# A tile of its own for the gate's normalized product, three weight stores moved from block 0 to block 1, and split z weights read back

## The chip, the cores and the metric

The kernel runs on one core of a Trainium2 chip. The metric is the device time of one execution in microseconds (us), the median of several runs.

## What is computed

One layer of a streaming encoder, for 2048 new prompt frames and 32 frames of a running stream (with 2048 cached keys and values). Cut to what matters here:

```python
def mixer(h, k_past, v_past, ssm_h0, conv_prev, p):
    proj = h @ p['w_in']                       # q, k, v, z, xbc, dt
    ...
    attn = stick_breaking(q, q_pos, k_all, v_all, k_pos).reshape(b, l, D_ATT)
    xbc_c, conv_new = causal_dwconv(xbc, conv_prev, p['ssm_conv_w'], p['ssm_conv_b'])
    xbc_c = jax.nn.silu(xbc_c)                 # x (4 tiles of 128), B, C
    ...
    y, h_fin = ssd_scan(xh, dt, a, bm, cm, ssm_h0.astype(jnp.float32))
    y = y + p['d_skip'].astype(jnp.float32)[:, None] * xh
    y = rmsnorm(y * jax.nn.silu(z), p['g_ssm_out'])      # the gate
    out = jnp.concatenate([rmsnorm(attn, p['g_attn_out']), y], axis=-1) @ p['w_out']
    return out, k, v, h_fin.astype(ssm_h0.dtype), conv_new

def layer(x, ...):
    x = x + rmsnorm(mixer(rmsnorm(x, p['g_mix_pre']), ...), p['g_mix_post'])
    x = x + rmsnorm(conv_ffn(rmsnorm(x, p['g_ffn_pre']), ...), p['g_ffn_post'])
```

## The kernel before

Frames lie along the free axis, features on the 128 partitions. The 2080 frames are cut into four blocks (`SBS`): 512, 512, 512 and 544 frames, numbered 0 to 3 (`s`).

Precision. Every fp32 operand of a matmul is split into a high part (rounded to fp32r) and a low part (the rest), and three matmuls (high x high, high x low, low x high) make one product; `dense` (L169) issues them. A weight that comes from its input tensor is loaded raw (L130), the high part is a cast on ScalarE (ACT, L153) and the low part a subtraction on GpSimd (POOL, L154), both in `divide`. If `divide` is given a key, the split pair is stored to a scratch tensor in device memory (L157), and the next `weight` call with that key reads it back with one load (`recall`, L145). A split pair has twice the bytes of the raw weights. All loads and stores are issued by SyncE (SP) in one order.

The input phase (`phase_in`) handles the four blocks one after another, with weight units of 8 chunks of 128 x 128, three buffers for split pairs and two for raw weights. In a block it projects tiles 4 and 5 (B and C), then 0 to 3 (x), each followed by the causal convolution on VectorE (DVE, L400, L404) into `bc` or `xc` and a SiLU (L384 on ACT, L385 on DVE); `xc` has one buffer, used by all blocks in turn. The copies of the projections out of PSUM (L393, L395) are on ACT. Then come V (L428; its weights `wvhi`, `wvlo` are split while block 0 runs, L291 and L292; copies L435 and L437), the state scan (L506 to L580), K and Q (L169; copy L360, split L602, L603), and the gate: `gate` multiplies the scan's output in `xc` with SiLU of the z projection (L652), `gate_norm` takes the root mean square (L663 to L667, `rstd`), multiplies by it (L672, in place in `xc`), splits the product (`khi` L676 on ACT, `klo` L678 on POOL) and stores both parts (L679, L680).

Block 3's `gate` and `gate_norm` are not run in the input phase: they are the filler of the attention of block 0 (`heads`), one step per slot. From there on weight units are of 4 chunks, with six buffers for split pairs and five for raw weights. In a slot PE makes scores (L885, L889), ACT two sigmoids (L733, L734), DVE a product scan (`prow`, L736), POOL or DVE a product (L741), PE transposes (L904) and the product with V (L926). The 32 frames of the running stream (`sample`, L759 to L800) are woven in, with their own loads of cached keys and values. PE's order is fixed here by pins between neighbours (`pin`, `mark`); the order on other engines, and in the input phase on all, comes from the scheduler of the framework, which lays out the whole program at compile time by simulating it.

The attention of block s + 1 is then woven with the output projection and the feed-forward network of block s (`Tail`). The change doesn't touch these.

Of the kernel before, what the change touches and what calls it, by code (L numbers as in the profile page):

```python
# [8 lines left out]
F32 = mybir.dt.float32  # L9
# [3 lines left out]
ALU = mybir.AluOpType  # L13
# [5 lines left out]
UNIT = 4  # L19
# [12 lines left out]
P = 128  # L32
# [13 lines left out]
NSB = len(SBS)  # L46
# [6 lines left out]
C_GSSM = 36  # L53
# [12 lines left out]
def tiles_of(n):  # L66
    return [(0, n)] if n <= 512 else [(0, n // 2), (n // 2, n)]


class Kernel:  # L70
# [69 lines left out]
    def recall(self, pool, keys, m, tag=None):  # L140

        w = self.held(pool, tag)
        q = m // len(keys)
        for i, k in enumerate(keys):
            self.nc.sync.dma_start(w[:, :, q * i : q * i + q, :].bitcast(F32), self.kept[k][:])  # L145
        return [(w[:, 0, i, :], w[:, 1, i, :]) for i in range(m)]

    def divide(self, pool, raw, m, key=None, tag=None):

        nc = self.nc  # L150
        w = self.held(pool, tag)
        hi, lo = w[:, 0, :m, :], w[:, 1, :m, :]
        nc.scalar.copy(hi, raw[:, :m, :])  # L153
        nc.gpsimd.tensor_tensor(lo, raw[:, :m, :], hi.bitcast(F32), op=ALU.subtract)  # L154
        if key is not None:
            d = self.kept[key] = self.dp.tile([P, 2, m, P], F32, name="wS_" + "_".join(map(str, key)))
            nc.sync.dma_start(d[:], w[:, :, :m, :].bitcast(F32))  # L157
        return [(w[:, 0, i, :], w[:, 1, i, :]) for i in range(m)]

    def parts(self):  # L160
# [19 lines left out]
    def rstd(self, pool, psp, sq, n, width, tag="rstd", pt="st"):  # L180
        nc = self.nc
        r = pool.tile([P, 544], F32, name=tag)
        for c0, c1 in tiles_of(n):
            ps = psp.tile([P, 512], F32, name=pt)
            nc.tensor.matmul(
                ps[:, : c1 - c0], self.ones[:], sq[:, c0:c1], start=True, stop=True
            )
            nc.scalar.activation(
                r[:, c0:c1], ps[:, : c1 - c0], AF.Sqrt, bias=self.eps[:], scale=1.0 / width
            )  # L190
        nc.vector.reciprocal(r[:, :n], r[:, :n])
        return r
# [68 lines left out]
def phase_in(kn, ctx):  # L261
    nc, tc, a, o = kn.nc, kn.tc, kn.a, kn.o
# [7 lines left out]
    wp = kn.wp  # L270
# [88 lines left out]
        else:  # L359
            nc.scalar.copy(dst, ps)  # L360

    wfirst = kn.weight(wp, a["wbx"][4], key=("bx", 4))
    for s, (t0, nt) in enumerate(SBS):
        last = s == NSB - 1
        if s == 0:
# [6 lines left out]
        xc = kn.xcp.tile([P, 4, 547], F32, name="xc")  # L372
# [9 lines left out]
        def silu(y, copy):  # L382
            t = tmp.tile([P, 550], F32, name="t")
            kn.behind(nc.scalar.activation(t[:, :W], y, AF.Sigmoid), copy)  # L384
            nc.vector.tensor_tensor(y, y, t[:, :W], op=ALU.mult)  # L385

        for c in (4, 5, 0, 1, 2, 3):
            w = wfirst if s == 0 and c == 4 else kn.weight(wp, a["wbx"][c], key=("bx", c))
            for c0, c1 in tiles_of(nt):
                ps = psd.tile([P, 512], F32, name="o")  # L390
                kn.dense(ps, w, xs, c0, c1)
                e = min(c1, 512)
                copy = nc.scalar.copy(raw[:, c, 3 + c0 : 3 + e], ps[:, : e - c0])  # L393
                if c1 > 512:
                    copy = nc.scalar.copy(raw[:, c, 518:550], ps[:, e - c0 : c1 - c0])  # L395
            if s == 0:
                nc.vector.tensor_tensor(raw[:, c, 3 : 3 + nt], raw[:, c, 3 : 3 + nt], r0[:, :nt], op=ALU.mult)
            y = xc[:, c, :W] if c < 4 else bc[:, c - 4, :W]
            wc = C_SW + c * 4
            nc.vector.tensor_scalar(  # L400
                y, raw[:, c, 0:W], kn.col(wc), kn.col(C_SB + c), op0=ALU.mult, op1=ALU.add
            )
            for i in range(1, 4):
                nc.vector.scalar_tensor_tensor(  # L404
                    y, raw[:, c, i : i + W], kn.col(wc + i), y, op0=ALU.mult, op1=ALU.add
                )
            if owed is not None:
                silu(owed, copy)
            owed = y
# [12 lines left out]
        for b in range(nb):  # L422
            q = min(P, nt - b * P)
# [67 lines left out]
        for b in range(nb):  # L491
            q = min(P, nt - b * P)
# [12 lines left out]
            for h in range(NH):  # L505
                nc.vector.tensor_scalar(  # L506
                    acB[:q, h, :q], acB[:q, h, :q], acum[:q, b * 8 + h : b * 8 + h + 1], 0.0,
                    op0=ALU.subtract, op1=ALU.min,
# [82 lines left out]
        for name, dst in (("wk", kn.kS), ("wq", kn.qS)):  # L591
            for c in range(4):
                w = kn.weight(wp, a[name][c])
                hi = so.tile([P, 544], F32, name="khi")[:].bitcast(F32R)
                lo = so.tile([P, 544], F32, name="klo")[:].bitcast(F32R)
                kf = so.tile([P, 544], F32, name="kf")
                for c0, c1 in tiles_of(nt):
                    ps = psd.tile([P, 512], F32, name="o")
                    kn.dense(ps, w, xs, c0, c1)
                    n = c1 - c0  # L600
# [13 lines left out]
        if last:  # L614
            return lambda tm, pool: (
                gate(kn, s, xs, xc, None, tm),
                gate_norm(kn, s, xc, tm, lambda sq, *r: kn.rstd_narrow(pool, *kn.bank, [sq], *r)),
            )
        bufs = {"khi": 2, "klo": 2, "t": 2, "sq": 1, "zc": 2}
        tm = lambda nm: (so if nm in ("khi", "klo") else tmp).tile([P, 550 if nm == "t" else 544], F32, name=nm, bufs=bufs[nm])  # L620
        for _ in gate(kn, s, xs, xc, r0 if s == 0 else None, tm):
            pass
        for _ in gate_norm(kn, s, xc, tm, lambda *r: kn.rstd(rp, psm, *r, tag="rstd2")):
            pass


def gate(kn, s, xs, xc, r0, tm):

    nc, nt = kn.nc, SBS[s][1]
    tiles = tiles_of(nt)  # L630
    for c in range(4):
        w = kn.weight(kn.wp, kn.a["wz"][c], key=("z", c) if s < NSB - 1 else None)
        for c0, c1 in tiles:
            n = c1 - c0
            ps = kn.po.tile([P, 512], F32, name="o")
            for k in range(KC):
                kn.dense(ps, w[k : k + 1], xs, c0, c1, k0=k, first=k == 0, last=k == KC - 1, pin=s == NSB - 1)
                if len(tiles) == 1 or k % 2:
                    yield
            t = tm("t")  # L640
            if r0 is not None:
                z = tm("t")
                nc.vector.tensor_tensor(z[:, :n], ps[:, :n], r0[:, c0:c1], op=ALU.mult)
                ps = z
            elif s < NSB - 1:
                z = tm("zc")
                nc.scalar.copy(z[:, :n], ps[:, :n])
                ps = z
            nc.scalar.activation(t[:, :n], ps[:, :n], AF.Sigmoid)
            nc.vector.tensor_tensor(t[:, :n], ps[:, :n], t[:, :n], op=ALU.mult)  # L650
            e = min(c1, 512)
            nc.vector.tensor_tensor(xc[:, c, c0:e], xc[:, c, c0:e], t[:, : e - c0], op=ALU.mult)  # L652
            if c1 > 512:
                nc.gpsimd.tensor_tensor(xc[:, c, 512:544], xc[:, c, 515:547], t[:, e - c0 : n], op=ALU.mult)


def gate_norm(kn, s, xc, tm, rstd):

    nc, nt = kn.nc, SBS[s][1]
    sq = tm("sq")  # L660
    for c in range(4):
        if c == 0:
            nc.scalar.activation(sq[:, :nt], xc[:, c, :nt], AF.Square)  # L663
        else:
            t = tm("t")
            nc.scalar.activation(t[:, :nt], xc[:, c, :nt], AF.Square)
            nc.gpsimd.tensor_tensor(sq[:, :nt], sq[:, :nt], t[:, :nt], op=ALU.add)  # L667
        yield
    r = rstd(sq, nt, 512)
    for c in range(4):  # L670
        yield
        nc.vector.scalar_tensor_tensor(  # L672
            xc[:, c, :nt], xc[:, c, :nt], kn.col(C_GSSM + c), r[:, :nt], op0=ALU.mult, op1=ALU.mult
        )
        hi = tm("khi")[:, :nt].bitcast(F32R)
        nc.scalar.copy(hi, xc[:, c, :nt])  # L676
        lo = tm("klo")[:, :nt].bitcast(F32R)
        nc.gpsimd.tensor_tensor(lo, xc[:, c, :nt], hi.bitcast(F32), op=ALU.subtract)  # L678
        nc.sync.dma_start(kn.yS[s][0, :, c, :], hi.bitcast(F32))  # L679
        nc.sync.dma_start(kn.yS[s][1, :, c, :], lo.bitcast(F32))  # L680

# [281 lines left out]
class Tail:  # L963
# [187 lines left out]
    def sums(self, j, gate, up):  # L1151


        kn, nc = self.kn, self.kn.nc
        (a11, a12), (a21, a22) = gate, up
        op = lambda out, a, b, o: nc.vector.tensor_tensor(out[:], a[:], b[:], op=o)
        op(a11, a11, a21, ALU.subtract)
        op(a21, a21, a22, ALU.add)
        op(a22, a22, a11, ALU.subtract)
        op(a12, a12, a22, ALU.subtract)  # L1160
        return {7: a11, 5: a21, 6: a22, 3: a12}
# [332 lines left out]
def build(nc, tc, a, o):  # L1494
    kn = Kernel(nc, tc, a, o)
    with ExitStack() as ctx:
# [17 lines left out]
        with ExitStack() as c2:  # L1514
            kn.wp, kn.unit, kn.wbufs, kn.rbufs = c2.enter_context(tc.tile_pool(name="weights_in", bufs=1)), KC, 3, 2
            rest = phase_in(kn, c2)
# [125 lines left out]
```

## Time and profile before

| | before |
|---|---|
| median of 3 runs | 2924.41 us (2918.09 to 2925.8) |
| the profiled execution | 2923.97 us |
| its span, first to last instruction | 2922.2 us |
| mean granted TensorE clock | 0.981 |
| PE busy | 2808.3 us (96%) |
| DVE busy | 1667.7 us (57%) |
| ACT busy | 1246.6 us (43%) |
| POOL busy | 1203.1 us (41%) |
| moved by DMA | 610.59 MB |

The profiled execution is a run of its own; its time stands beside the span because some microseconds lie before the first and after the last instruction. A row of a timeline gives the start, the duration, the engine, the line, the operation, out<-in, shapes and how many are merged, and in brackets the idle time of the engine before it with what ended it. PE is TensorE's matmuls, PEld its weight loads. A row of waits gives who waited for whom: total, times, longest.

### The profile page before, as it was taken

Reading aid. Unit: us, or ns where it says so; the run is one execution under the profiler, and the core shown is the slowest. Engines: PE = TensorE matmul, PEld = TensorE weight load, DVE = VectorE, ACT = ScalarE, POOL = GpSimd, SP = SyncE. Lnnn points to the kernel's source line nnn. Section 1 sums busy time; section 2 is a strip of 40 time slices with the busy share of each in tenths; the row PEclk is TensorE's granted clock in tenths of the full one; section 3 lists DMA queues with packets and bytes.
Section 4 is the critical chain, followed back from the end, with each engine's and each line's share of the span. In section 5 each row is a group of like instructions: output and inputs, shape, how many; then the busy total and the mean of one; then the engine's idle time right before and its main releaser. Section 6 shows DMA issues by size and latency. Waiting matters only on the chain.

```text
span 2922.2 us, 46225 instructions
## 1 busy us (share of the span) xinstructions
PE 2808.3 (96%) x16771; PEld 2428.2 (83%) x16771; DVE 1667.7 (57%) x2628; ACT 1246.6 (43%) x2604; POOL 1203.1 (41%) x1105
## 2 busy tenths in 40 slices
PE   7999999989989999999999999989999999999998
PEld 6787878877878888897788888978888889899997
DVE  7666666557574555457555556676656663623333
ACT  4344344337565454455333334654444443321111
POOL 4535252335666666656322323453322223511113
PEclk9999999989889999999999999999999999999999
DMA  7766665658777778776755556666555555755556
GB/s 263 206 234 196 222 174 201 173 139 283 242 249 267 258 265 272 262 266 225 232 172 175 178 184 221 216 194 204 169 171 171 164 163 201 244 176 175 171 177 204
DMA packets 334533, 610.59 MB, mean 209 GB/s; under 512 B 73466, under 2 KB 192898, under 8 KB 329698
## 3 DMA queue, kind: packets, MB, share of 16 engines
q1 hardware_dynamic: 334306, 607.64, 64.2%
q8 instruction: 134, 2.20, 0.3%
q14 instruction: 93, 0.76, 0.1%
HBM read 459.33 MB, written 148.18 MB: 208 GB/s over the span
## 4 chain that ended last, share of the span: by engine, by line
PE 77%; DVE 10%; DMA 7%; issue 2%; ACT 2%; SPq 1%; POOL 1%; DVEq 0%; POOLq 0%; ACTq 0%
PE o L169 38%; PE u L169 12%; PE t L169 10%; PE z L885 4%; PE pa L926 4%; PE pt L904 3%; PE o L428 3%; DVE acB L506 1%; DVE xc L404 1%; DMA xr<-hS 1%; DVE prow L736 1%; DVE xc L560 1%; DMA w<-wS_up 1%; DMA acB<-acD 1%; DVE xlo L1074 1%
## 5 line engine op out<-in xcount | busy, mean ns | idle before, releaser
L169 PE MATMUL o<-xhi,w 128*128 128x512 f32 (+2 forms) x3968 | 1050.4, 346 | 21.8 <-ACT xhi L342 7.8
L169 PEld LDWEIGHTS o<-xhi,w 128*128 128x128 f32 x3968 | 700.8, 192 | 115.0 <-ACT xhi L342 7.8
L169 PE MATMUL o<-xlo,w 128*128 128x512 f32 (+2 forms) x1984 | 684.7, 345 | 2.1 <-DVE xlo L343 1.1
L741 POOL TENSOR_TENSOR beta<-beta,prow 128x512 f32<-128x512 f32 (+3 forms) x256 | 253.4, 991 | 450.0 <-DVE prow L736 376.1
L169 PEld LDWEIGHTS o<-xlo,w 128*128 128x128 f32 x1984 | 380.7, 192 | 45.1 <-DVE xlo L343 1.6
L154 POOL TENSOR_TENSOR w<-wraw,w 128x512 fp32r<-128x512 f32 (+3 forms) x218 | 313.9, 1443 | 206.9 <-ACT w L153 186.0
L169 PE MATMUL u<-xhi,w 128*128 128x512 f32 x1056 | 350.1, 397 | 0.0
L169 PE MATMUL o<-ah,w 128*128 128x512 f32 x992 | 344.1, 403 | 4.6 <-DVE f L1370 3.8
L1322 POOL TENSOR_TENSOR y<-y,gb 128x512 f32<-128x512 f32 (+1 forms) x88 | 115.9, 1317 | 503.1 <-ACT gb L1321 503.0
L736 DVE TENSOR_TENSOR_SCAN prow<-gam,prow,z 128x513 f32<-128x513 f32 x192 | 245.2, 1278 | 72.5 <-ACT beta L734 69.5
L909 DVE TENSOR_TENSOR wt<-pt,wt 128x512 fp32r<-128x512 f32 (+2 forms) x320 | 190.9, 602 | 160.1 <-ACT wt L908 158.4
L908 ACT CAST wt<-pt 128x512 fp32r<-128x512 f32 (+2 forms) x320 | 166.9, 527 | 222.2 <-PE pt L904 220.4
L169 PEld LDWEIGHTS u<-xhi,w 128*128 128x128 f32 x1056 | 199.2, 189 | 46.9
L169 PEld LDWEIGHTS o<-ah,w 128*128 128x128 f32 x992 | 187.0, 189 | 47.1 <-DVE f L1370 5.7
L153 ACT CAST w<-wraw 128x512 fp32r<-128x512 f32 (+3 forms) x218 | 145.1, 666 | 166.9 <-PE o L169 111.5
L733 ACT ACTIVATE gam<-z 128x512 f32<-128x512 f32 (+2 forms) x320 | 172.6, 539 | 95.2 <-PE z L885 54.8
L169 PE MATMUL u<-xlo,w 128*128 128x512 f32 x528 | 209.5, 397 | 0.0
L169 PE MATMUL o<-al,w 128*128 128x512 f32 x496 | 196.6, 396 | 0.0
L169 PE MATMUL t<-xhi,w 128*128 128x272 f32 x960 | 187.4, 291 | 2.6 <-DMA w<-wS_up 1.7
L904 PE MATMUL pt<-ident,beta 128*128 128x128 f32 x1088 | 181.3, 279 | 3.0 <-DVE beta L741 1.8
L1314 DVE SCALAR_TENSOR_TENSOR y<-gb,cv,y 128x512 f32<-128x512 f32 (+1 forms) x176 | 142.1, 808 | 73.4 <-ACT y L1312 70.7
L926 PE MATMUL pa<-wt,v 128*64 128x256 f32 (+3 forms) x1152 | 174.6, 282 | 8.9 <-DVE wt L909 6.8
(282 smaller groups left out, 4924.5 us busy)
## 6 DMA issues: line engine op xcount, KB each, us to landing
w<-wS_up SPq DMA_DIRECT2D x264, 512.0 KB, 3.6
w<-wS_dn SPq DMA_DIRECT2D x144, 384.0 KB, 3.5
wS_up<-w SPq DMA_DIRECT2D x88, 512.0 KB, 3.5
w<-wS_out SPq DMA_DIRECT2D x78, 512.0 KB, 5.8
wraw<-wup SPq DMA_DIRECT2D x88, 256.0 KB, 4.3
k<-kS SPq DMA_DIRECT2D x80, 256.0 KB, 4.0
v<-vS SPq DMA_DIRECT2D x80, 256.0 KB, 3.8
w<-wS_bx SPq DMA_DIRECT2D x18, 1024.0 KB, 4.8
```

Source lines behind the costliest of these rows:

```text
L153: nc.scalar.copy(hi, raw[:, :m, :])
L154: nc.gpsimd.tensor_tensor(lo, raw[:, :m, :], hi.bitcast(F32), op=ALU.subtract)
L169: mm = nc.tensor.matmul(ps[:, : c1 - c0], l, r, start=first and i == 0 and k == 0, stop=last and i == 2 and k == len(w) - 1, **({"skip_gro ...
L733: nc.scalar.activation(g[:, c0:512], z, AF.Sigmoid, scale=-0.125)
L736: nc.vector.tensor_tensor_scan(back(pr), back(g), z[:, 0:1].to_broadcast([P, n + 1]), self.kn.ones[:, 0:1] if prev is None else prev, op0= ...
L741: eng.tensor_tensor(b[:, :n], b[:, :n], pr[:, c0 + 1 : 513], op=ALU.mult)
L885: mm = nc.tensor.matmul(z[:, :n], q[:, P * b : P * b + P], k[:, :n], start=e == 0, stop=e == 1 and kc < s)
L904: mm = nc.tensor.transpose(t[:, P * j : P * j + P], w[:, P * j : P * j + P], kn.ident[:])
L908: nc.scalar.copy(hi, t)
L909: nc.vector.tensor_tensor(lo, t, hi.bitcast(F32), op=ALU.subtract)
L926: nc.tensor.matmul(av[:m, 2 * P * p + c0 : 2 * P * p + 2 * P], v[:, j, :m], wt[:, rest, j, c0:], start=kc == s and p + j + rest == 0, stop ...
L1314: nc.vector.scalar_tensor_tensor(y[:, :W], gb[:, i : i + W], kn.col(wc + i), y[:, :W], op0=ALU.mult, op1=ALU.add)
```

## The change

Three edits. The normalized product in `gate_norm` goes, for blocks 0 to 2, to a tile of its own (`zc`, two buffers) in place of `xc`; ACT and POOL read it there. The split weights of tiles 4, 5 and 0 of the B/C/x projection get no key in block 0, so they aren't stored there; block 1 loads them raw, splits them again and stores them, and blocks 2 and 3 read them back as before. Block 3's z weights, loaded raw and split in units of 4 chunks before, are read back as halves of the units of 8 chunks that block 0 stored; for that, `divide` also notes the parts of a long unit under keys of their own.

```diff
@@ recall
-            self.nc.sync.dma_start(w[:, :, q * i : q * i + q, :].bitcast(F32), self.kept[k][:])
+            self.nc.sync.dma_start(w[:, :, q * i : q * i + q, :].bitcast(F32), self.kept[k])
@@ divide
-            d = self.kept[key] = self.dp.tile([P, 2, m, P], F32, name="wS_" + "_".join(map(str, key)))
+            d = self.dp.tile([P, 2, m, P], F32, name="wS_" + "_".join(map(str, key)))
             nc.sync.dma_start(d[:], w[:, :, :m, :].bitcast(F32))
+            self.kept[key] = d[:]
+            if m > UNIT:
+                for i in range(0, m, UNIT):
+                    self.kept[(*key[:-1], "part", i)] = d[:, :, i : i + UNIT, :]
@@ phase_in
-    wfirst = kn.weight(wp, a["wbx"][4], key=("bx", 4))
+    wfirst = kn.weight(wp, a["wbx"][4])
...
         for c in (4, 5, 0, 1, 2, 3):
-            w = wfirst if s == 0 and c == 4 else kn.weight(wp, a["wbx"][c], key=("bx", c))
+            w = wfirst if s == 0 and c == 4 else kn.weight(wp, a["wbx"][c], key=("bx", c) if s or c in (1, 2, 3) else None)
@@ gate
     for c in range(4):
-        w = kn.weight(kn.wp, kn.a["wz"][c], key=("z", c) if s < NSB - 1 else None)
+        w = kn.weight(kn.wp, kn.a["wz"][c], key=("z", c) if s < NSB - 1 else ("z", c, "part"))
@@ gate_norm
     for c in range(4):
         yield
+        n = xc[:, c, :nt] if s == NSB - 1 else tm("zc")[:, :nt]
         nc.vector.scalar_tensor_tensor(
-            xc[:, c, :nt], xc[:, c, :nt], kn.col(C_GSSM + c), r[:, :nt], op0=ALU.mult, op1=ALU.mult
+            n, xc[:, c, :nt], kn.col(C_GSSM + c), r[:, :nt], op0=ALU.mult, op1=ALU.mult
         )
         hi = tm("khi")[:, :nt].bitcast(F32R)
-        nc.scalar.copy(hi, xc[:, c, :nt])
+        nc.scalar.copy(hi, n)
         lo = tm("klo")[:, :nt].bitcast(F32R)
-        nc.gpsimd.tensor_tensor(lo, xc[:, c, :nt], hi.bitcast(F32), op=ALU.subtract)
+        nc.gpsimd.tensor_tensor(lo, n, hi.bitcast(F32), op=ALU.subtract)
```

## The prediction, made before the changed kernel ran

> **What bounds the kernel now.** I read the page's first part, then the waits of TensorE (PE) over the stages that the change touches, then a table of windows.
>
> ```profile
> span 2922.2 us, 46225 instructions
> PE 2808.3 (96%) x16771; PEld 2428.2 (83%) x16771; DVE 1667.7 (57%) x2628; ACT 1246.6 (43%) x2604; POOL 1203.1 (41%) x1105
> ```
>
> PE is busy for 96% of the span, so the kernel is PE's queue of matmuls, and another engine's work costs time only where PE waits for it. The three edits lie in the first 770 us. PE's waits for the input phase (0 to 620 us), in total, times and longest:
>
> ```profile
> PE o L169 <- POOL w L154: 3.8, 2, 2.4
> PE o L428 <- ACT v L437: 3.3, 2, 2.4
> PE o L428 <- ACT raw L393: 3.2, 1, 3.2
> ```
>
> These are the rows that this change can reach: a weight that is split late (L154), and ScalarE (ACT) copies that come late to free a PSUM bank (L437, L393). Windows (busy us of PE, PEld, DVE, ACT, POOL, then granted clock, DMA share, GB/s):
>
> ```profile
> 24.00:37.00 13.00, 13.00 (x65) 10.72 (x64) 6.92 (x11) 4.51 (x6) 3.44 (x2) 1.00 1.03 397
> 37.00:43.00 6.00, 2.01 (x6) 1.04 (x6) 6.00 (x7) 1.53 (x2) 3.02 (x1) 0.82 0.58 240
> 43.00:48.00 5.00, 5.00 (x13) 3.90 (x13) 4.63 (x7) 4.59 (x6) 1.66 (x1) 0.53 0.90 303
> 35.00:70.00 35.00, 30.37 (x167) 25.53 (x165) 33.78 (x39) 14.57 (x20) 14.09 (x6) 0.90 0.65 226
> 150.00:197.00 47.00, 47.00 (x223) 37.62 (x222) 30.87 (x44) 20.51 (x31) 10.86 (x7) 1.00 0.71 260
> 367.00:373.00 6.00, 5.89 (x36) 5.89 (x37) 5.85 (x11) 1.26 (x4) 2.35 (x2) 0.72 0.48 115
> 626.00:640.00 14.00, 9.99 (x60) 8.48 (x58) 6.75 (x14) 8.41 (x21) 7.64 (x14) 0.88 0.44 111
> 640.00:668.00 28.00, 25.87 (x174) 20.37 (x173) 17.68 (x30) 19.61 (x54) 14.68 (x18) 0.88 0.85 269
> ```
>
> **Part 1: three stores fewer in block 0.** Tiles 4, 5 and 0 of the B/C/x weights are no longer stored while the chip starts up: three stores of 1,024 KB. From 24 to 37 us the DMA engines are full (share 1.03). The chain shows the raw weights of tile 2 under way for 13.2 us, and the timelines what waits for them:
>
> ```profile
> 24.17 13.20 DMA wraw<-wbx
> 37.97 1.05 ACT L153 CAST w<-wraw 128x1024 fp32r<-128x1024 f32 x1
> ...
> 39.07 0.50 PE L169 MATMUL o<-xhi,w 128*128 128x512 f32 x1 [1.62 <-ACT w L153]
> 42.17 1.22 PE L169 MATMUL o<-xhi,w 128*128 128x512 f32 x2 [2.37 <-POOL w L154]
> 18.98 0.33 SPq L157 DMA_DIRECT2D wS_bx<-w  x1
> 23.71 0.41 SPq L157 DMA_DIRECT2D wS_bx<-w  x1
> ```
>
> Two of the dropped stores stand in the queue just ahead of that load, 2.1 MB; at 397 GB/s they are 5.3 us. The load lands at 32.1 instead of 37.4, the cast and the POOL subtraction (1.05 us, and 3.02 in the next fence) end at 36.2, and PE wants the weights at 39.07 - 1.62 = 37.4: both waits go, 4.0 us. The clock of the next windows (0.82 over 6 us, 0.53 over 5 us) costs another 1.1 + 2.4 = 3.4 us. But the end of this stretch is not PE's. VectorE (DVE) is busy 33.78 of the 35 us from 35 to 70, and PE's V matmuls wait for its last piece of wvlo:
>
> ```profile
> 62.25 0.39 PE L428 MATMUL o<-wvlo,xhi 128*128 128x260 f32 x1 [0.64 <-DVE wvlo L292]
> 37.24 0.74 DVE L404 SCALAR_TENSOR_TENSOR xc<-raw,cv,xc 128x512 f32<-128x512 f32 x1
> 39.83 2.83 DVE L404 SCALAR_TENSOR_TENSOR xc<-raw,cv,xc 128x512 f32<-128x512 f32 x1
> 39.09 3.02 POOL L154 TENSOR_TENSOR w<-wraw,w 128x1024 fp32r<-128x1024 f32 x1 [10.11 <-ACT w L153]
> ```
>
> So what PE saves at 37 is mostly waited away at 62, unless K matmuls are put ahead there. What DVE itself saves is one collision: the same operation takes 0.74 us alone and 2.83 us under the subtraction, and at about 33 us that subtraction meets a DVE that has hardly begun. Bounds 0 and 7.4 us (4.0 + 3.4); I take 2, the 2.1 us of that collision, because the DVE row is the nearest.
>
> **Part 2: the normalized product in a tile of its own.** Each block's last step multiplies xc in place and splits it by ACT and POOL; the next block's convolution writes xc and waits for the last subtraction:
>
> ```profile
> 205.25 3.55 DVE L400 TENSOR_SCALAR xc<-raw,cv 128x512 f32<-128x512 f32 x3 [5.67 <-POOL klo L678]
> 506.64 3.10 DVE L400 TENSOR_SCALAR xc<-raw,cv 128x547 f32<-128x547 f32 x2 [5.14 <-POOL klo L678]
> 197.28 3.25 POOL L678 TENSOR_TENSOR klo<-xc,khi 128x512 fp32r<-128x512 f32 x2 [14.36 <-ACT khi L676]
> 494.47 3.25 POOL L678 TENSOR_TENSOR klo<-xc,khi 128x512 fp32r<-128x512 f32 x2 [10.18 <-ACT khi L676]
> 505.32 1.28 POOL L678 TENSOR_TENSOR klo<-xc,khi 128x512 fp32r<-128x512 f32 x1 [4.41 <-DMA yS<-klo]
> ```
>
> PE pays at one remove: ACT's SiLU waits for the convolution, and the copies that free PE's banks are queued behind it on ACT.
>
> ```profile
> 365.44 1.35 ACT L384 ACTIVATE t<-xc 128x512 f32<-128x512 f32 x2 [5.50 <-DVE xc L404]
> 216.56 0.39 PE L428 MATMUL o<-wvhi,xhi 128*128 128x260 f32 x1 [0.82 <-ACT v L437]
> 367.11 0.39 PE L428 MATMUL o<-wvhi,xhi 128*128 128x260 f32 x1 [2.44 <-ACT v L437]
> 517.16 0.39 PE L428 MATMUL o<-wvhi,xhi 128*128 128x260 f32 x1 [3.20 <-ACT raw L393]
> 349.81 0.58 ACT L393 COPY raw<-o 128x512 f32<-128x512 f32 x1
> 502.20 0.19 ACT L395 COPY raw<-o 128x32 f32<-128x32 f32 x1
> ```
>
> After the change xc is free once DVE's fourth product is made. The change adds a wait there: the new tile has two buffers, so products three and four wait for the first and second POOL subtraction, and DVE's later work is queued behind them. In block 3 those two end at 494.47 + 3.25 = 497.7, and the convolution's own input (L395) is there at 502.4, 4.2 us before the present start at 506.64. In block 2 the input is there at 350.4; in block 1 the second subtraction ends at 197.28 + 3.25 = 200.5, so 4 us of the 5.67 go. Each lead is longer than the PE wait behind it, so all three waits go: 0.82 + 2.44 + 3.20 = 6.5 us. Behind the second the clock is 0.72 for 6 us, 1.7 us of PE; I count it too. Bounds 0 and 8.2; I take 8.2. Next late is the scan (L518), which starts from PE's V work and moves with it.
>
> The Trainium skill's page "TensorE: Matmul & The Clock Gate", Part 1, says that the clock is halved after an idle window of about 3.4 us. Here 2.44 us of idle is followed by a low clock, so the trace is stricter than the page; by the page's rule the 1.7 us would not be part of the sum, which would then be 8.5.
>
> **Part 3: the same three tiles are split again in block 1.** Three casts of 1.05 us and three subtractions of up to 3.02 us, most of them before 197 us, where ACT is busy 20.51 and POOL 10.86 of 47 us and PE never waits. Loads shrink from 1,024 to 512 KB each and three stores come in at DMA share 0.71. SP is no worse: a raw load doesn't wait for PE to free a split buffer, a recall does. Hidden, except that each subtraction can hold a DVE operation for 2.1 us (above); DVE is busy 30.87 of 47. Bounds 0 and 3 x 2.1 = 6.3 us of cost; I take 1, because only the chain to the last product is tight.
>
> The Trainium skill's page "SBUF — State Buffer" (the shared port) says that GpSimd and a VectorE operation with two SBUF inputs lock each other out for the whole instruction. The 0.74 and 2.83 us agree. By that rule with no slack on DVE, Part 3 costs its full 6.3 us.
>
> **Part 4: the last block's z weights are loaded split.** Eight units lose a cast and a subtraction; each load becomes 512 KB instead of 256 KB, with as many issues on SP.
>
> ```profile
> L153 ACT CAST w<-wraw x8: 619/660/690, 630.7 to 661.2; 128x512 fp32r<-128x512 f32 x8
> L154 POOL TENSOR_TENSOR w<-wraw,w x8: 1274/1286/1289, 631.4 to 666.0; 128x512 fp32r<-128x512 f32 x8
> PE z L885 <- DVE prow L736: 5.3, 6, 2.1
> SPq L145 <- PE o L169: 12.2, 3, 6.0
> ```
>
> That frees 8 x 0.66 = 5.3 us of ACT and 8 x 1.29 = 10.3 us of POOL, neither of which is full there (640 to 668: 19.61 and 14.68 of 28). PE waits for the scan of the scores (third row, 626 to 770 us), which stands behind ACT's sigmoids; two of the eight casts stand ahead of one. The price is 2.1 MB more, 7.8 us of transfer at 269 GB/s, in windows with DMA shares of 0.44 and 0.85, so about 7.8 + 4.2 us are free. Gain at most 5.3 us, loss as in the slower rival; I take a gain of 1, two casts of 0.66 us.
>
> **The sum.** 2 + 8.2 - 1 + 1 = 10.2 us less. The profiled execution took 2923.97 us (span 2922.2), 0.4 below the median of 2924.41, so 2924.4 - 10.2 = 2914 us.
>
> **Rivals.** (a) The start comes back whole, because K matmuls fill the stretch before 62 us: 7.4 + 8.2 - 1 + 1 = 15.6, so 2909. For it: PE, not DVE, is full again after 70. Against it: 33.78 of 35.
> (b) The wait for xc only changes its name: with two buffers DVE sits 3.25 us behind two subtractions, the backlog stays, and one us is won at each of three blocks, nothing at the start: 2921. For it: the second subtraction ends at 497.7 and the split of C is behind it. Against it: the leads of 4 us above.
> (c) Slower: the split z loads wait on SP for a free buffer, as recalls do now (fourth row: three waits, 6.0 us the longest, 180 to 205 us), and the attention's K, Q and cache loads behind them on SP come late while PE's order there is fixed. Each such wait that reaches PE costs 6.0 us; it decides from three on (18 us against the 8.2 of Part 2): 2924.4 - 8.2 + 18 = 2934. For it: DMA share 0.85. Against it: six buffers for eight loads, so the first six needn't wait.
>
> **Chances.** The forecast 0.52, with its own range of 2910 to 2918; (a) 0.17, (b) 0.22, (c) 0.09. Of this kernel about 0.3%, 8.8 us, can be told from no change: below 2915.6 lie (a) and two thirds of the forecast, 0.52; the rest of it and (b) are the same, 0.39; (c) is slower, 0.09. The range goes from all upper bounds, 7.4 + 8.2 + 5.3 = 20.9 us or 2903, to no gain with 1 us of cost, 2925.
>
> **What would show it.** Right: the convolution's idle for klo under 1.5 us in blocks 1 to 3, and no PE wait on L437 and L393; tile 2's raw load under 9 us and no PE wait at 37; L154 213 times in place of 218 (three more, eight fewer). Part 1's doubt is told by PE's wait on wvlo: several us mean that DVE kept the gain. Wrong: the order of instructions is laid out again at compile time, so a new order on ACT or DVE could hold a copy back in a place that this trace doesn't show; and PE's waits in 626 to 770 us could grow with the loads.

## The result, and the profile after

The changed kernel takes 2934.49 us (median of 6 runs, 2931.63 to 2941.92); the kernel before took 2921.46 us beside it (6 runs). The ratio is 1.0049, 95% interval 1.0038 to 1.0061: slower by 0.5%, some 13 us, where 2914 was forecast. The profiled execution took 2931.63 us.

The page of the changed kernel, first part (busy time, share of the span, instructions):

```profile
span 2929.9 us, 46191 instructions
...
PE 2807.0 (96%) x16771; PEld 2427.6 (83%) x16771; DVE 1678.5 (57%) x2628; ACT 1244.4 (42%) x2599; POOL 1208.6 (41%) x1100
...
L154 POOL TENSOR_TENSOR w<-wraw,w 128x512 fp32r<-128x512 f32 (+3 forms) x213 | 313.2, 1473 | 226.9 <-ACT w L153 194.7
```

PE does the same work (2807.0 against 2808.3 us), so the loss is waiting. DVE is 10.8 us busier with the same number of instructions. L154 is there 213 times, as forecast.

To find the place I took, for each kernel, the time at which PE has started the same amount of matmul work, and subtracted the kernel before. What each stretch of the kernel before adds to the difference, in us of one profiled execution (minus is ahead):

```
                       0-50  50-150  150-210  210-610  610-900  900-1330  1330-1480  1480-end
changed kernel         -6.8    +5.1     +6.4     -7.8     +4.1      +1.5      +10.4      -5.1
```

The start is won and given back, 6.4 us are lost in block 1, the stretch with the three transitions (the points where a block's gate hands `xc` to the next block's convolution) wins 7.8, the beginning of the attention loses 4.1, and the largest loss, 10.4 us, lies at 1330 to 1480 us, in code that the diff does not touch. (The last column differs by several us between any two runs of this kernel.)

The windows and PE's waits of the changed kernel in the early stages (line numbers are 4 or 5 higher than before):

```profile
37.00:43.00 6.00, 6.00 (x27) 4.81 (x27) 5.16 (x8) 2.50 (x3) 2.00 (x1) 1.00 0.91 376
43.00:48.00 5.00, 5.00 (x23) 3.96 (x22) 5.00 (x5) 2.82 (x3) 2.43 (x2) 1.00 0.77 252
35.00:70.00 35.00, 28.20 (x166) 24.89 (x165) 33.87 (x41) 13.60 (x19) 15.04 (x6) 0.95 0.60 216
150.00:197.00 47.00, 42.08 (x194) 33.03 (x191) 35.34 (x41) 21.98 (x31) 17.58 (x10) 1.00 0.74 263
```

```profile
PE o L432 <- DVE wvlo L296: 4.3, 1, 4.3
...
PE y L520 <- DVE bc L389: 2.5, 1, 2.5
PE o L173 <- DMA w<-wS_bx: 2.2, 1, 2.2
PE o L173 <- DVE xlo L332: 1.8, 1, 1.8
PE o L432 <- ACT v L441: 1.5, 2, 1.1
```

At 37 us PE no longer waits and the clock is whole. From 35 to 70 us DVE is still full (33.87 of 35), and PE hands the time back at DVE's bc and wvlo. From 150 to 197 us PE was full before and is now busy 42.08 of 47. The transitions, and the attention's beginning:

```profile
352.26 0.55 DVE L404 TENSOR_SCALAR xc<-raw,cv 128x512 f32<-128x512 f32 x1
...
499.76 0.56 DVE L404 TENSOR_SCALAR xc<-raw,cv 128x547 f32<-128x547 f32 x1
```

```profile
PE z L789 <- DMA sk<-kF: 7.0, 1, 7.0
```

The convolution of blocks 2 and 3 starts without an idle time for klo (and so in block 1, at 202.77 us). The wait of 7.0 us for the decode step's K load is new.

The stage with the largest loss, first in the kernel before, then in the changed one (windows: PE, PEld, DVE, ACT, POOL, granted clock, DMA share, GB/s):

```profile
1355.00:1375.00 20.00, 20.00 (x99) 16.54 (x98) 11.05 (x15) 9.37 (x22) 14.01 (x17) 1.00 0.56 187
...
1395.00:1415.00 20.00, 17.24 (x83) 14.46 (x82) 12.10 (x24) 6.61 (x17) 8.17 (x9) 0.91 0.75 231
1415.00:1435.00 20.00, 19.27 (x93) 15.40 (x93) 10.29 (x15) 9.88 (x22) 5.92 (x6) 1.00 0.80 258
```

```profile
1355.00:1375.00 20.00, 15.60 (x74) 12.53 (x73) 17.99 (x25) 9.59 (x26) 13.55 (x17) 0.91 0.66 198
...
1395.00:1415.00 20.00, 14.89 (x72) 12.00 (x72) 12.18 (x24) 6.77 (x17) 9.48 (x7) 0.98 0.50 164
1415.00:1435.00 20.00, 17.52 (x72) 14.70 (x73) 16.21 (x22) 6.49 (x14) 9.79 (x9) 0.76 0.53 161
```

PE's waits of the changed kernel from 1330 to 1480 us (in total, times, longest):

```profile
PE o L173 <- DVE f L1375: 4.7, 3, 3.6
PE z L890 <- DVE rn_v L232: 4.3, 1, 4.3
PE pa L931 <- DVE wt L914: 2.7, 2, 2.5
```

All three are put down to DVE, and DVE's own timeline says what it was doing (start, us, what, in brackets its idle time before and the releaser):

```profile
1403.48 0.41 DVE L1411 TENSOR_TENSOR f<-f,xr 128x256 f32<-128x256 f32 x1
1408.89 0.43 DVE L1411 TENSOR_TENSOR f<-f,xr 128x256 f32<-128x256 f32 x1 [5.00 <-DMA xr<-hS]
...
1412.60 0.43 DVE L1411 TENSOR_TENSOR f<-f,xr 128x256 f32<-128x256 f32 x1 [2.69 <-DMA xr<-hS]
...
1413.54 1.27 DVE L741 TENSOR_TENSOR_SCAN prow<-gam,prow,z 128x513 f32<-128x513 f32 x1
1414.73 0.13 DVE L232 SCALAR_TENSOR_TENSOR rn_v<-u,rcol 128x2 f32<-128x2 f32 x1
```

The scan (`prow`) and rn_v stand in DVE's queue behind adds of `finish` (L1411, L1406 in the kernel before). These wait for their residual xr, which SP loads behind a store that itself waits for an add. PE goes on at 1414.87 us. The row of waits names rn_v, which ends last, but the waiting matmul does not read it; it writes one of two PSUM banks that the scans read, and this scan ends 0.05 us before rn_v, so the scan is the likelier cause.

In the kernel before, the same adds waited too (13.7 us in all, 14.7 now), and rn_v stood behind the third of them as it does now:

```profile
1397.34 0.43 DVE L1406 TENSOR_TENSOR f<-f,xr 128x256 f32<-128x256 f32 x1 [2.07 <-DMA xr<-hS]
1397.68 0.15 DVE L228 SCALAR_TENSOR_TENSOR rn_v<-u,rcol 128x2 f32<-128x2 f32 x1
```

What has moved is the scan: in the kernel before this one ran at 1436.66 us, behind all eight of DVE's adds, the last of which ran at 1421.17.

No Python line of this stage changed. Its order is made by the compile step, which simulates the whole program and lays each engine's queue out by what it thinks is ready. In the compiled programs, among the 18,758 instructions written after the last block's gate, 591 of DVE's 1,836 stand elsewhere than before, and 4,252 of PE's 12,533.

### The profile page after: what moved, and what is told of

Read it like the earlier page. It is cut to its first block, busy times and chain, and to the rows that moved or that the text cites. A ratio compares the mean times of both kernels' runs of the same rounds, so it can differ in the third digit from the quotient of the medians.

```text
span 2929.9 us, 46191 instructions
## 1 busy us (share of the span) xinstructions
PE 2807.0 (96%) x16771; PEld 2427.6 (83%) x16771; DVE 1678.5 (57%) x2628; ACT 1244.4 (42%) x2599; POOL 1208.6 (41%) x1100
## 4 chain that ended last, share of the span: by engine, by line
PE 78%; DVE 9%; DMA 6%; issue 2%; ACT 2%; SPq 1%; POOL 1%; DVEq 0%; POOLq 0%; ACTq 0%
PE o L173 38%; PE u L173 12%; PE t L173 11%; PE z L890 4%; PE pa L931 4%; PE pt L909 4%; PE o L432 3%; DMA acB<-acD 1%; DVE acB L510 1%; DVE prow L741 1%; DMA wraw<-wbx 1%; DVE xlo L1079 1%; DVE xc L564 1%; DVE xc L408 1%; DMA w<-wS_out 1%
## 5 line engine op out<-in xcount | busy, mean ns | idle before, releaser
L154 POOL TENSOR_TENSOR w<-wraw,w 128x512 fp32r<-128x512 f32 (+3 forms) x213 | 313.2, 1473 | 226.9 <-ACT w L153 194.7
L931 PE MATMUL pa<-wt,v 128*64 128x256 f32 (+3 forms) x1152 | 172.8, 281 | 12.1 <-DVE wt L914 10.8
```

The lines of the kernel that those rows point to most:

```text
L931: nc.tensor.matmul(av[:m, 2 * P * p + c0 : 2 * P * p + 2 * P], v[:, j, :m], wt[:, rest, j, c0:], start=kc == s and p + j + rest == 0, stop ...
```

## The experiments

**Theory (order):** the order laid out anew costs some 10 us at 1330 to 1480 us, the three edits little. **Rival (data flow):** the moved stores, the second split and the z loads cost it, whatever the order.

An order can be held: at the end of `build` each engine's late instructions (those 18,758) are chained, without waits, in a list taken from another compiled program:

```
+    for ins, prev in ...:   # neighbours on one engine, in the order of the list
+        tc.add_manual_dep(ins, prev.name, NoSync, reason="follow")
```

"Late order as before" means this list from the kernel before. The kernel before was timed beside each set: 2924.03 us (e1 to e4), 2920.97 (e5 to e8), 2922.70 (e9 to e12). Ratios are to it, as recorded; they are not quite the quotients of the two medians (for e6 that would be 0.9945 in place of 0.9953). The differences by stretch, as above, of all of them:

```
                         0-50  50-150  150-210  210-610  610-900  900-1330  1330-1480  1480-end
e1  all, order before    -7.2    +5.5     +7.9     -6.2     +4.9      -0.0       +0.3      +2.2
e2  none, order after    +0.0    +0.1     +0.0     +1.3     -1.5      +1.8      +12.1      +1.6
e3  zc alone             +0.1    +0.2     +0.0     -5.6     +0.9      +1.9       +2.2      +4.8
e4  z loads alone        +0.1    +0.2     +0.0     +1.0     +2.1      +0.0       +2.3      +2.9
e5  all, xr early        -6.9    +6.9     +8.5     -1.2     +3.6      +1.5       +6.5      -8.1
e6  zc, xr early         -0.2    +0.3     +0.0     -2.5     -5.6      -0.0       -5.0      -9.9
e7  stores moved alone   -6.7    +6.0     +6.6     +2.3     -6.5      -0.0       +2.5      +3.0
e8  z loads, sk first    +0.2    +0.3     -0.0     +1.4     +1.8      +0.0       +0.5      -2.2
e9  xr early alone       +0.3    +0.5     -0.0     +4.0     -1.8      -0.1       -4.4      -9.1
e10 z loads, free order  +0.3    +0.3     +0.0     +4.7     +0.2      +1.3      +12.1      -3.0
e11 second split alone   -1.1    -0.8     +3.3     +1.7     +1.1      +0.1       -0.4      -2.8
e12 zc, xr x4, free      -0.9    +0.5     -0.0     +0.5     +0.2      -0.1       -3.4      +2.1
```

One execution stands behind each row; where nothing was changed, rows differ by up to 8 us (610-900: -6.5 in e7, +1.1 in e11), so only what repeats in several rows counts.

### e1 and e2: the edits and the order, crossed

e1 is the changed kernel with the late order as before.

> The changed kernel, all edits kept; every engine is made to issue what was written after the last block's gate (from the last normalisation to the end of the kernel) in the order of the kernel before. Theory (order): the loss of some 12 us at 1340 to 1410 us, in a stage that the diff does not touch, comes from the order that was laid out anew there at compile time, so the kernel comes to 2918 to 2924 us against 2921 before, and the wait for f (L1375) and for rn_v at 1410 us are gone. Rival (data flow): the loss is made by the moved stores, the second split and the z loads, whatever the late order: 2931 to 2937 us, as the changed kernel's 2934.5.

Measured: 2928.73 us, ratio 1.0015 (0.9999 to 1.0030). PE's waits from 1330 to 1480 us:

```profile
PE u L250 <- POOL rn_v L238: 2.7, 1, 2.7
PE z L890 <- DVE prow L741: 1.9, 2, 1.1
PE o L173 <- DVE f L1375: 1.7, 2, 1.0
```

e2 is the kernel before, with none of the edits, in the changed kernel's late order.

> The kernel before, none of the edits; every engine is made to issue what was written after the last block's gate in the order of the changed kernel. Theory (order): 2929 to 2934 us, 8 to 12 above the kernel before, lost at 1340 to 1410 us with PE waiting for DVE's f. Rival (data flow): 2919 to 2924 us, no change.

Measured: 2940.48 us, ratio 1.0051 (1.0035 to 1.0067). Its waits in the same stretch, with the kernel before's line numbers:

```profile
PE z L885 <- DVE rn_v L228: 4.9, 1, 4.9
PE o L169 <- DVE f L1370: 4.7, 3, 3.5
PE pa L926 <- DVE wt L909: 2.3, 2, 2.1
```

The order alone loses as much as the changed kernel, with the same three waits, and more than the 8 to 12 us expected; without it the loss at 1330 us is 0.3 us. So the order was the cause of most of the loss. The edits seem to keep a cost of their own: e1 was expected at 2918 to 2924 us, level with the kernel before, and is about 4 us slower, though its interval just reaches no change. The two costs, 0.15% and 0.51%, sum to more than the 0.49% of both together; with intervals of 0.15% each way that is no contradiction.

### e10: which edit turns the order over

The z loads alone, nothing held:

```
-        w = kn.weight(..., key=("z", c) if s < NSB - 1 else None)
+        w = kn.weight(..., key=("z", c) if s < NSB - 1 else ("z", c, "part"))
```

> The kernel before with the z loads edit alone, and nothing held: the order is the one that the compile step lays out by itself. Of VectorE's 1,836 late instructions 587 stand elsewhere than before (591 in the changed kernel; 76 differ between these two). Theory (order, laid out anew because of the z loads): 9 to 13 us lost at 1330 to 1480 us, beside the 2 to 5 us at 610 to 720: about 1.004 to 1.006 times the kernel before. Rival (it takes all three edits): under 4 us lost there, 1.000 to 1.002.

Measured: 2939.33 us, ratio 1.0065 (1.0053 to 1.0078); 12.1 us lost at 1330 to 1480 us. The theory holds, and the total is a little above its range. In the compiled programs the other two edits turn DVE's order far less: zc alone moves 130 of its 1,836 late instructions, the moved stores 6. No run measured what the order of either of these costs by itself.

### e5, e6, e9, e12: is it DVE held up by xr?

The edit is in `finish`, and on SP each load of xr stands where the load two before it stood:

```
-                h = att.tmp.tile([P, 272], F32, name="xr", bufs=2)[:, :n]
+                h = att.tmp.tile([P, 272], F32, name="xr", bufs=4)[:, :n]
```

e5 does that to the changed kernel and holds all else in its own order.

> The changed kernel, the order of every engine held as it is there, but for the loads of xr (L1401 of the kernel before, the residual that finish adds): four buffers for two, and on SP each load stands where the load two earlier stood. Theory (VectorE held up by xr): at 1400 to 1445 us DVE's add f<-f,xr waits in order for its load (15.9 us there in the run of the order alone) and what PE waits for, the scan and rn_v, is queued behind it; with the loads early those waits on xr fall under 5 us, PE's wait of 4.3 us for rn_v at 1410 goes with its low clock of 0.76, and the kernel gains 6 to 9 us: about 1.002 to 1.003 times the kernel before, where it was 1.005. Rival (f and xlo): the new order loses by f and xlo being late at 1350 to 1370 us, where DVE is full, and the xr loads don't matter: 1.004 to 1.006 as the changed kernel.

Measured: 2931.68 us, ratio 1.0033 (1.0021 to 1.0044). From 1330 to 1480 us the loss is 6.5 us, not 10.4, and PE's wait for rn_v is 1.3 us, not 4.3. The other half is still there:

```profile
1355.00:1375.00 20.00, 13.92 (x65) 10.29 (x65) 20.00 (x31) 14.08 (x36) 13.71 (x14) 0.94 0.62 199
```

At 1355 us DVE is full for all 20 us: the new order puts xlo and scans ahead of f, which frees PE's banks. So theory and rival each had a part: xr makes about 4 us at this place. Of the rest the rows show PE's waits on f, 4.7 us where the kernel before has 1.7, and on wt, 3.0 us where it has 0.2; no run took either away by itself.

e6 gives the early xr loads to the kernel with zc alone, late order as before.

> The kernel before with the tile of its own for gate's product (zc) alone, the late order held as before, and the same early loads of xr in four buffers. If zc's 6 us at the three transitions are kept and DVE's waits of 13.7 us on xr at 1385 to 1421 us cost PE something before, too: 8 to 12 us below the kernel before. If DVE's waits there were hidden: 3 to 6 us below, as zc alone. Rival: the four loads together delay the weights on SP and PE waits for w: no gain.

Measured: 2904.95 us, ratio 0.9953 (0.9935 to 0.9972): the fastest of all, some 14 us below the kernel before. Who waited for xr at 1340 to 1480 us, in the kernel before and then here:

```profile
DVE f L1406: 13.7, 6
POOL f L1406: 9.9, 6
```

```profile
DVE f L1407: 1.5, 3
```

PE's wait for POOL's rn_v goes with it, first in the kernel before, then here:

```profile
PE u L246 <- POOL rn_v L234: 2.8, 1, 2.8
```

```profile
PE u L246 <- POOL rn_v L234: 0.3, 1, 0.3
```

POOL's part of rn_v starts from DVE's, and DVE's stood behind adds that waited for xr (the row at 1397.34 us above is the last of them). The next block's `finish`, at 1900 to 2000 us, has the same wait: 3.2 us in the kernel before, none here and in e9, 0.2 in e5. From 1965 to 1975 us alone these three runs win 4.0 to 4.2 us; the others lie between 1.0 won and 1.4 lost. The prediction did not look at these stages, though the early loads alone won some 10 us in all (e9, next), more than the 8.2 forecast for the largest of the edits.

e9 takes zc out again and keeps the xr loads:

> The kernel before, its order held on every engine, with the early loads of xr in four buffers alone (no zc). It tells what zc adds to the run of both, which was 0.9953 of the kernel before. If the early loads made most of it (by the trace of that run 5 us at 1330 to 1480, and up to 10 at 1900 to 2600 us): 8 to 14 us below the kernel before, zc adding 2 to 6. If zc made most of it: 0 to 4 us below.

Measured: 2910.81 us, ratio 0.9965 (0.9953 to 0.9977). The loads make most of the gain. What zc adds to it, 0.12%, is within the intervals.

e12 has zc and four buffers, with nothing held:

> The kernel before with zc and with four buffers for xr, nothing held: two edits of a line, and the compile step places the loads by itself. In its order the first four loads of xr stand ahead of the first store, and later ones in pairs behind two stores. If buffers are what the loads lacked: within 5 us of the version held by hand (0.9953). If the place on SP is what counts, or the order laid out anew costs as it did in the changed kernel: 0.998 to 1.003.

Measured: 2917.49 us, ratio 0.9978 (0.9966 to 0.9990): half of the gain, between the two expectations. The adds of the first `finish` still wait 13.7 us for xr on DVE and POOL together, where the kernel before has 23.6 and e9 1.2, and in the next block's `finish` PE's wait for rn_v is 3.0 us, as before. So four buffers alone do not bring the loads in time, and their place on SP counts beside the buffers. What the rest of the order, laid out anew here too, adds or takes is not separated.

### e3, e7, e11: the edits one by one

e3 is zc alone, late order as before.

> The kernel before with one edit alone: gate's normalised product in a tile of its own (zc); the late order is held as it was before. By the three transitions (0.82 + 2.44 + 3.20 us of waits and 1.7 of clock): 2912 to 2915 us, 6.5 to 9 below the kernel before. Rival (given back): what the transitions win is waited away at the next fixed point, the loads of the attention at 630 us: 2920 to 2922 us.

Measured: 2923.52 us, ratio 0.9991 (0.9977 to 1.0005). PE wins 5.6 us from 210 to 610 us. Over the runs with zc (changed, e1, e3, e5, e6, e12) that stretch stands at -3.8 on average, over those without at +2.3: the edit wins 6 us there. The total is about 2.6 us better, which the interval does not tell from nothing, so the expected 6.5 to 9 us did not come; in the profiled execution 9.9 us were lost after 610 us, in stretches that zc does not touch, and these differ from run to run.

e7 is the moved stores alone, late order as before (the diff's lines in `phase_in`).

> The kernel before with one edit alone: the three tiles stored, and so split again, in block 1 and not 0; the late order held as before. Theory (shared time of VectorE and GpSimd): at 100 us PE is 1.3 us ahead, at 200 us 5 to 7 us behind, since each of the three subtractions on GpSimd holds one DVE operation 2.1 us longer; in all 4 to 6 us over the kernel before. Rival: what was lost at 165 to 200 us in the changed kernel came with zc: no more than 1 us behind at 200 us, and the time of the kernel before.

Measured: 2923.82 us, ratio 1.0010 (0.9999 to 1.0021). At 150 us it is 0.7 us ahead, and then 6.6 us are lost by 210 us, as in the three other runs with this edit (6.4 to 8.5; nothing in the runs without it, e11 apart). The place and the size there are as expected; the total, 3 us over, is a little under and at the edge of what the interval tells from nothing.

e11 tells the split from the stores: block 0 stores as before, and block 1 splits tiles 4, 5 and 0 again without storing.

```
+            ... key=("bx", c) if s != 1 or c in (1, 2, 3) else None)
```

> The kernel before, late order held; block 0 stores all six tiles as before, but block 1 loads tiles 4, 5 and 0 raw and splits them again, without storing them; blocks 2 and 3 load them split. No store is moved. Theory (GpSimd's subtraction holds VectorE): nothing changes before 150 us, and 5 to 7 us are lost at 150 to 210 us, as in the run with the stores moved (6.5 there); the scale at L318 and xlo at L328 take over 0.9 us each on average, not 0.75 and 0.68. Rival (the moved stores crowd the recalls of tiles 1 to 3, PE's wait of 2.2 us on w<-wS_bx): 0 to 2.5 us lost.

Measured: 2925.48 us, ratio 1.0009 (0.9997 to 1.0021); 3.3 us lost at 150 to 210 us, between the two. DVE's groups from 160 to 205 us, in the kernel before and then in e11 (count, busy us, mean ns):

```profile
L318 DVE SCALAR_TENSOR_TENSOR x<-x,cv,rstd 128x512 f32<-128x512 f32 x8 | 5.4, 748 | 0.0
L328 DVE TENSOR_TENSOR xlo<-x,xhi 128x512 fp32r<-128x512 f32 x8 | 5.2, 684 | 0.0
```

```profile
L328 DVE TENSOR_TENSOR xlo<-x,xhi 128x512 fp32r<-128x512 f32 x8 | 8.9, 1153 | 0.0
L318 DVE SCALAR_TENSOR_TENSOR x<-x,cv,rstd 128x512 f32<-128x512 f32 x8 | 7.5, 1011 | 0.0
```

and PE's waits of e11 from 150 to 210 us:

```profile
PE o L169 <- DVE xlo L328: 1.8, 1, 1.8
PE o L169 <- DVE t L643: 0.9, 1, 0.9
```

The split takes 5.8 us of DVE, and PE waits 2.7 us for it. The rest, some 3 to 5 us, comes only with the moved stores: PE's wait on w<-wS_bx, 2.2 to 2.7 us in the four runs with them, is not there in e11. So both theories had a half.

### e4 and e8: the z loads

e4 is the z loads alone, late order as before.

> The kernel before with one edit alone: the last block's z weights loaded split; the late order is held as it was before. Theory (order): the loads themselves cost little once the late order stays: 2919 to 2923 us. Rival (data flow): the longer loads on SP hold the attention's cache and K loads back, PE waits 4 to 7 us at 632 us: 2925 to 2929 us.

Measured: 2925.73 us, ratio 1.0008 (0.9993 to 1.0023). PE's waits from 610 to 720 us:

```profile
PE z L788 <- DMA sk<-kF: 7.0, 1, 7.0
PE z L889 <- DVE prow L740: 2.7, 2, 2.1
```

On SP the first load of sk now stands behind eight loads of qp, which take 4.92 us to issue; in the kernel before it stood ahead of them. e8 puts it back (`behind` holds each of the eight qp loads behind it).

> As the run of the z loads alone (late order as before), but with the first load of sk held ahead of the eight loads of qp on SP, as it stood in the kernel before. Theory (one load's place in the queue): PE's wait of 7.0 us for sk at 632 us goes, PE is level with the kernel before at 700 us (it was 4.8 us behind), and the time is that of the kernel before within 2 us. Rival (longer transfers): the 512 KB z loads themselves hold the attention's loads back, and the wait stays at 4 us or more.

Measured: 2927.90 us, ratio 1.0019 (1.0008 to 1.0030). The same stretch:

```profile
PE z L892 <- DVE prow L740: 4.6, 5, 2.1
PE z L791 <- DMA qp<-qF: 2.4, 1, 2.4
```

The wait for sk is gone and the time with it is not: qp is late instead, and prow takes 4.6 us again, as in the kernel before. Both expectations failed. That the z loads cost something here does repeat: from 610 to 720 us alone the six runs with them lose 4.6 to 6.9 us (e8 6.0), and the seven without lie between 1.5 won and 2.7 lost. By 900 us the averages are 2.8 lost and 1.9 won. What makes this loss of some 5 us stays open: one load's place does not.

## Why the prediction was wrong

The forecast was 10.2 us of gain and the kernel lost 13. Three steps of it failed: the new order of later stages had no term in the sum, and cost most; Part 3 took 1 us where 7 were lost; Part 4 had the wrong sign.

**Part 1 (forecast gain 2): right.** Without the three stores PE's waits and the low clock at 37 us go, 7 us by 50 us, and come back at wvlo (0.64 us before, 4.3 now) because DVE was full. At 150 us the four runs with it are 0.0 to 1.7 us ahead, about 1 us on average. Its test came out: a wait on wvlo of several us meant that DVE kept the gain.

**Part 2 (forecast gain 8.2): right in kind, 6 us in size.** The convolution no longer waits for klo, and no PE wait on the copy of raw is left. One sign failed in part: PE still waits 1.5 us for the copy of v, where it waited 3.3.

**Part 3 (forecast cost 1): mis-sized, 7.4 us over four runs.** Two sentences failed. "Only the chain to the last product is tight" took 1 from a range up to 6.3: DVE lost 5.8 us of those 6.3, in the scale and in xlo, which PE's next matmuls stand behind. PE was full there before, and 3.3 us of its time went with it (e11); 1 was too little. The Trainium skill's page "SBUF — State Buffer", section "SBUF: two separate sides", says that a GpSimd operation that reads SBUF and a VectorE operation with two SBUF inputs shut each other out. e11 agrees: beside the three subtractions xlo goes from 684 to 1,153 ns on average.

The other sentence is "SP is no worse". It overlooked that the three stores come in ahead of the recalls of tiles 1 to 3; with them the loss is 7.4 us, above the upper bound of 6.3.

**Part 4 (forecast gain 1): wrong in sign.** Some 5 us are lost at 610 to 720 us in every run with the z loads. In e4 and in the changed kernel PE's longest wait there is of rival (c)'s kind, a K load late on SP, though the queue before it was the eight qp loads and not z loads waiting for a buffer. But e8 took that wait away and the loss stayed, so its cause is open.

**The sum.** The four parts come to -1 - 6 + 7 + 5, some 5 us of loss, and e1 measures about 4. So even with the order unchanged the forecast of 10.2 us of gain would have failed, by Part 3 and Part 4.

**What was left out: the order.** The larger part is the late order: 10 to 12 us at 1330 to 1480 us, and 0.51% in all when it is alone (e2). The prediction named it as a thing that could make it wrong ("a new order on ACT or DVE could hold a copy back in a place that this trace doesn't show") and gave it neither a price nor a chance; it also looked for losses only in the first 770 us. What was held back was not a copy but DVE's f, a scan and wt. Rival (c)'s 2934 us equals the measured time, but by chance: a late load on SP made at most some 5 of its 18 us.

## What to carry to other kernels

Where a compile step orders the queues, an edit that changes a load's kind is also a throw for the order of every later stage: hold the old order to see what the edit itself does, and give a new order a price, here 0.5%. A queue that issues in order should not hold an operation that waits for a load ahead of one that the bottleneck waits for; loading that operand two places earlier won 0.35%, as much as the three edits were forecast to win together. Where the bottleneck engine is full, the cost of work on an engine next to it is not near zero: here PE lost 3.3 of the 5.8 us that the split took from DVE.

## What was not expected of the hardware

The granted clock after an idle time of TensorE is not a function of that idle time alone. In the changed kernel and in e1 PE waits for the same xlo, 1.78 and 1.77 us, just before 180 us. The window behind it, first in the changed kernel, then in e1:

```profile
180.00:190.00 10.00, 10.00 (x44) 8.07 (x43) 7.23 (x10) 4.09 (x7) 4.13 (x3) 1.00 0.71 253
```

```profile
180.00:190.00 10.00, 10.00 (x38) 7.97 (x37) 5.69 (x10) 3.58 (x6) 3.86 (x3) 0.84 0.69 223
```

The clock is 1.00 in the one and 0.84 in the other, with 44 and 38 matmuls recorded in 10 us. The other three runs with this wait (1.77 to 1.78 us) divide too: 1.00 in e7 and e11, 0.83 in e5. The Trainium skill's page "TensorE: Matmul & The Clock Gate", Part 1, gives an idle window of about 3.4 us ahead of a halved clock. The traces of e1 and e5 show a low clock behind half of that, those of the changed kernel, e7 and e11 do not.
